# The down projection's seven products in the order 1 5 6 3 2 7 4, with the norms of the first token half issued in steps among the last two

## The chip, the cores and the metric

The kernel runs on one core of a Trainium2 chip. The metric is the device time of one execution in microseconds (us). A core has a matrix engine (TensorE, PE in the profile; PEld is its weight load), a vector engine (VectorE, DVE), a scalar engine (ScalarE, ACT), GpSimd (POOL) and a queue engine for transfers (SyncE, SP). They run side by side, each through its own list of instructions in order, and wait for one another through semaphores.

## The reference, cut to what matters

One layer of a decoder trunk, 512 tokens wide 1024, in float32:

```python
h = swiglu(rms_norm(x, ffn1_pre), ffn1_w_gu, ffn1_w_down)     # D_FF = 2816
x = x + 0.5 * rms_norm(h, ffn1_post)
h = token_mixer(rms_norm(x, mix_pre), ...)                    # pooling groups and sliding-window attention
x = x + rms_norm(h, mix_post)
h = swiglu(rms_norm(x, ffn2_pre), ffn2_w_gu, ffn2_w_down)
x = x + 0.5 * rms_norm(h, ffn2_post)

def rms_norm(x, g):  return x * rsqrt(mean(x * x, -1) + EPS) * g
def swiglu(h, w_gu, w_down):
    gate, up = split(h @ w_gu, 2);  return (silu(gate) * up) @ w_down
```

## The kernel before

**Precision.** A float32 product is made of three fp32r matmuls (`mm3`, L357 to L361): every operand is split into a high part (a cast on ACT) and a low part (a subtraction on DVE), and high x high, high x low and low x high are summed. So each chunk of weights costs a cast `f_d_hi` (L166) on ACT and a subtraction `f_d_lo` (L169) on DVE, and each operand made of activations costs the same (`f1e_hi`, `f1e_lo` at L635 and L636; the names begin with f1 in the first FFN and f2 in the second).

**The down projection** (`down_proj`, L616) multiplies 512 tokens x 2816 by 2816 x 1024. Both are cut in halves, and the four output quarters come from seven products in place of eight (Strassen's way with Winograd's sums). The products have numbers; `PRODUCTS` (L39) is their order, 1 5 6 3 7 2 4 before. A product covers 256 tokens (two blocks of 128, t = 0 and 1) by 512 columns, with an inner length of 1408: 11 slices of 128, in six chunks of weights (five of two slices, the last of one). A slice is three matmuls for each of the two blocks, so a product is 66 matmuls of 512 columns.

The products accumulate in PSUM banks, one for each block: 1, 6, 7 and 4 in `xs_` (f_x in the profile), one on top of the other, 5 and 3 in `ys` (f_y), and 2 in `zs_` (f_z). What the sums need from an intermediate state is taken off by `put_away` (L654): after 1, 5 and 6 copies on ACT, after 3, 7 and 2 a DVE instruction for each block. At the end the first token half (blocks 0 and 1) has its two column halves in kept[1] (the first product plus product 2) and kept[6]; the second half (blocks 2 and 3) has them in xs_ after product 4 and in kept[5].

The activations' operand for product i is made by `form(i, g)` in three groups g (two of four slices, one of three). For 5, 6, 3 and 7 a DVE instruction first combines two quarters in place (L626 to L632); for 1, 2 and 4 there is none. Then ACT casts and DVE subtracts.

**Order.** Inside `in_order()` PE, DVE, ACT and POOL run exactly in program order. For product i and chunk n that order is: weights of the chunk three ahead (cast and subtraction), at n = 0, 2, 4 the forming of a group of the next product, the chunk's matmuls, and at n = 0 the put-away of the product before. The weights' parts have six buffers, so the cast of a chunk waits until PE is through with the chunk six before it. Outside `in_order()` PE is still in program order, but DVE, ACT and POOL are placed by a planner. SP issues the transfers in program order.

**The end of the down projection.** Before the change `in_order()` covers the first six products. Then come two chunks of product 4 for both blocks, put_away(2) after the first, `normed(0)` and `normed(1)`; the other four chunks (the tail) run once for block 0 and once for block 1, each followed by `normed(2)` or `normed(3)`.

`normed(t)` (L672) is `post_norm` (L407): two squares with sums on ACT (`squares`, L353), the mean on DVE (L339), the root on POOL (L334), two multiplies by the gain on DVE (L413) that for t < 2 write in place over what the squares read, and two updates of x on DVE (L416). In the second FFN each update is followed by its transfer to the output on SP (L418). After that `done(t)` is called: nothing in the second FFN; in the first it is `done1` (L842), which is the mixer's `pre_norm` (L383) of the new x: squares on ACT, mean, root, two DVE instructions that write `xn_b` (L378).

`between(t)` is `between1` (L846) in the first FFN: eight transposes of xn_b on PE (`tr_mx`, L391) for t = 0 and 1, and copies of high and low parts into `xT` (L397 on ACT, L400 on DVE). Before the change between(0) comes between the two runs of the tail, and between(1) after the second chunk of block 1's run. The mixer then starts with `qkv_block(0)`: 24 matmuls of pq for block 0 of the tokens (xT and the weights wq), then 24 half as wide of pkv (weights wkv, cast when pkv asks for them).

Of the kernel before, what the change touches and what calls it, by code (L numbers as in the profile page):

```python
# [33 lines left out]
EPS = 1e-6  # L34
# [1 line left out]
CH = 256  # L36
NCH = FF // CH
TAIL = 4
PRODUCTS = (1, 5, 6, 3, 7, 2, 4)  # L39
BLOCKS = {1: (0, 0), 2: (1, 0), 3: (1, 1)}  # L40
CW = 256 + 16 * NG + 8
WB = 6
# [25 lines left out]
def trunk_layer(  # L68
# [37 lines left out]
    def in_order():  # L106
        return tc.manual_schedule(engines={E.PE, E.DVE, E.Activation, E.Pool})

    def bank(name):
        return banks_of["pool"].tile([P, 512], F32, tag="ps", name=name)  # L110
# [4 lines left out]
    def slot(name, shape=(P, 512), dtype=F32):  # L115
        return slots_of["pool"].tile(list(shape), dtype, tag="h", name=name)
# [67 lines left out]
    W = Weights()  # L184
# [50 lines left out]
    def add_ffn(name, w_gu, w_down):  # L235
        for c in range(NCH):
            add_gate_up(name, w_gu, c)
        cut = w_down[0].rearrange("(q j p) n -> j p q n", j=2, p=P)
        for i in PRODUCTS:
            for q in range(0, NCH, 2):  # L240
# [90 lines left out]
    def power(ms, name):  # L331

        r = sm.tile([P, 1], F32, tag="r", name=f"r_{name}")
        nc.gpsimd.tensor_tensor(r, ms, half, ALU.pow)  # L334
        return r

    def mean_square(ss2, eps, name):
        ms = sm.tile([P, 1], F32, tag="ms", name=f"ms_{name}")
        nc.vector.scalar_tensor_tensor(ms, ss2[:, 0:1], eps, ss2[:, 1:2], ALU.add, ALU.add)  # L339
        return ms  # L340
# [30 lines left out]
    def sizes(t, name, split=False):  # L371
        return squares([xs[t][:, :512], xs[t][:, 512:]], ROOT, f"{name}{t}", split)

    def scaled(t, r, g, name, between=lambda: None, xn=None):
        xn = xn or [slot(f"xn_{name}{t}{n}") for n in range(2)]
        for n in range(2):
            at = slice(n * 512, (n + 1) * 512)
            nc.vector.scalar_tensor_tensor(xn[n], xs[t][:, at], r, g[n], ALU.mult, ALU.mult)  # L378
            if n == 0:
                between()  # L380
        return xn

    def pre_norm(t, g, name, xn=None):  # L383
        r = power(mean_square(sizes(t, name), EPS, f"{name}{t}"), f"{name}{t}")
        return scaled(t, r, g, name, xn=xn)

    def transposes(t, xn, xT, name):
        for h in range(2):
# [15 lines left out]
    def halves(g):  # L404
        return g[:, :512], g[:, 512:]

    def post_norm(t, parts, tmp, g, scale, name, dst=None):  # L407

        ss2 = squares(parts, ROOT / scale, f"{name}{t}")
        r = power(mean_square(ss2, EPS / (scale * scale), f"{name}{t}"), f"{name}{t}")  # L410
        for n in range(2):
            at = slice(n * 512, (n + 1) * 512)
            nc.vector.tensor_tensor(tmp[n], parts[n], g[:, at], ALU.mult)  # L413
        for n in range(2):
            at = slice(n * 512, (n + 1) * 512)
            nc.vector.scalar_tensor_tensor(xs[t][:, at], tmp[n], r, xs[t][:, at], ALU.mult, ALU.add)  # L416
            if dst is not None:
                nc.sync.dma_start(dst[:, at], xs[t][:, at])  # L418
# [197 lines left out]
    def down_proj(name, hs, ends, g_post, between, done):  # L616

        forms = {}  # L620

        def form(i, g):

            a11, a21, a12, a22 = (hs[g][:, f] for f in range(4))
            if i == 5:
                nc.vector.tensor_tensor(a21, a22, a21, ALU.subtract)  # L626
            elif i == 6:
                nc.vector.scalar_tensor_tensor(a11, a21, -1.0, a11, ALU.mult, ALU.subtract)
            elif i == 3:
                nc.vector.scalar_tensor_tensor(a21, a11, -1.0, a12, ALU.mult, ALU.subtract)  # L630
            elif i == 7:
                nc.vector.scalar_tensor_tensor(a11, a11, -1.0, a22, ALU.mult, ALU.subtract)  # L632
            src = {1: a11, 5: a21, 6: a11, 3: a21, 7: a11, 2: a12, 4: a22}[i]
            hi, lo = act_pair(f"{name}e{i}{g}", src.shape)
            nc.scalar.copy(hi, src)  # L635
            nc.vector.tensor_tensor(lo, src, hi.bitcast(F32), ALU.subtract)  # L636
            forms[i, g] = hi, lo

        ys, zs_, xs_ = ([bank(f"{name}_{b}{t}") for t in range(2)] for b in "yzx")
        fresh = {1: xs_, 5: ys, 2: zs_}  # L640
        into = {**fresh, 6: xs_, 3: ys, 7: xs_, 4: xs_}
        kept = {}

        def multiply(i, n, w, blocks=(0, 1)):
            for q in range(2 * n, min(2 * n + 2, NCH)):
                hh, hl = forms[i, q // 4]
                for t in blocks:
                    at = (slice(None), q % 4, slice(t * P, (t + 1) * P))
                    mm3(
                        into[i][t], (hh[at], hl[at]), tuple(part[:, q % 2] for part in w),  # L650
                        i in fresh and q == 0, q == NCH - 1, True,
                    )

        def put_away(i):  # L654

            if i in (1, 5):
                kept[i] = wk.tile([P, 2, 512], F32, tag="sg2", bufs=2, name=f"{name}_p{i}")
                for t in range(2):
                    nc.scalar.copy(kept[i][:, t], into[i][t])
            elif i == 6:  # L660
                kept[i] = [slots_of["pool"].tile([P, 512], F32, tag="k", bufs=2, name=f"{name}_p6{t}") for t in range(2)]
                for t in range(2):
                    nc.scalar.copy(kept[i][t], xs_[t])
            for t in range(2):
                if i == 3:
                    nc.vector.scalar_tensor_tensor(kept[6][t], ys[t], -1.0, kept[6][t], ALU.mult, ALU.subtract)
                elif i == 7:
                    nc.vector.scalar_tensor_tensor(kept[5][:, t], xs_[t], -1.0, kept[5][:, t], ALU.mult, ALU.subtract)
                elif i == 2:
                    nc.vector.tensor_tensor(kept[1][:, t], zs_[t], kept[1][:, t], ALU.add)  # L670

        def normed(t):  # L672
            first = kept[1][:, t] if t < 2 else xs_[t - 2]
            second = kept[6][t] if t < 2 else kept[5][:, t - 2]
            dst = out[0, t * P : (t + 1) * P, :] if name == "f2" else None
            tmp = slots_of["pool"].tile([P, 512], F32, tag="k", bufs=2, name=f"{name}_n{t}") if t >= 2 else first
            post_norm(t, [first, second], [tmp, second], g_post, 0.5, f"{name}po", dst)
            done(t)

        NW = (NCH + 1) // 2  # L680
        with behind(ends[0]):
            form(1, 0)
            form(1, 1)
        with behind(ends[1]):
            form(1, 2)
            W.get(f"{name}_d10")
        with in_order():
            for at, i in enumerate(PRODUCTS[:-1]):
                for n in range(NW):
                    w = W.get(f"{name}_d{i}{n}")  # L690
                    if n % 2 == 0:
                        form(PRODUCTS[at + 1], n // 2)
                    multiply(i, n, w)
                    if n == 0 and at:
                        put_away(PRODUCTS[at - 1])
        i = PRODUCTS[-1]
        for n in range(2):
            multiply(i, n, W.get(f"{name}_d{i}{n}"))
            if n == 0:
                put_away(PRODUCTS[-2])  # L700
        normed(0)
        normed(1)
        tail = [W.get(f"{name}_d{i}{n}", 0) for n in range(2, NW)]
        if name == "f1":
            W.run_ahead = 3
            W.more(2)
        for t in range(2):
            for n, w in enumerate(tail):
                multiply(i, n + 2, w, (t,))
                if t and n == 1:  # L710
                    between(1)
            if t and name == "f1":
                W.more(2)
            normed(t + 2)
            if t == 0:
                between(0)
        use_slots(f"{name}_end", HB)


# [67 lines left out]
    ends = gate_up("f1", xq, hs, first_steps)  # L787
    g2 = gain(ffn1_post, "g2")
    g3 = halves(gain(mix_pre, "g3"))
# [16 lines left out]
    late = ExitStack()  # L806
# [33 lines left out]
    xns = {}  # L840

    def done1(t):  # L842
        xn = ap.tile([P, 2, 512], F32, tag=("ahi", "alo")[t % 2], name=f"xn_b{t}")
        xns[t] = pre_norm(t, g3, "b", [xn[:, n] for n in range(2)])

    def between1(t):  # L846
        if t == 0:
# [364 lines left out]
    def normed(t):  # L1212
        later["x", t] = scaled(t, later["r", t], g5, "c")
# [68 lines left out]
    hs2 = []  # L1282
    ends = gate_up("f2", xq2, hs2, last_steps)
    g6 = gain(ffn2_post, "g6")
    down_proj("f2", hs2, ends, g6, lambda t: None, lambda t: None)


# [27 lines left out]
```

## Time and profile before

| | |
|---|---|
| median of three runs | 872.73 us (870.80 to 873.77) |
| the profiled execution, its own time | 870.79 us |
| its span in the profile | 869.0 us |
| PE busy, share of the span | 829.5 us, 95% |
| DVE busy | 686.1 us, 79% |
| ACT busy | 447.0 us, 51% |
| POOL busy | 234.1 us, 27% |
| mean granted clock of TensorE | 0.981 |

The first FFN's down projection lies from about 249 to 362 us of the span, the second's from about 752 to 862. Busy times are of engines that work side by side. A matmul row's duration reaches past the start of the next one, since matmuls are pipelined; the distance from start to start is what a matmul costs. In a timeline the brackets hold the idle time of the engine before the row and what ended it.

### The profile page before, as it was taken

The numbers are of one execution on the slowest core, as the hardware profiler recorded it, in microseconds if no ns is written. First come the engines' busy times: TensorE is split into PE (matmuls) and PEld (weight loads), VectorE is DVE, ScalarE is ACT, GpSimd is POOL, SyncE is SP. The second block draws the span as 40 slices with busy tenths as digits, with TensorE's granted clock in tenths as the row PEclk, the third lists the DMA queues.
The fourth block names the chain that finished last, engine by engine and source line by source line (L and its number), as shares of the span: only waits on it lengthen the run. The fifth ranks groups of instructions, "written<-read, shape, count | busy, mean of one in ns | idle before, by whom it ended". The sixth has DMA issues, their size and how long they took to land. (4 is left out here: it accounts for less than half of the span.)

```text
span 869.0 us, 13979 instructions
## 1 busy us (share of the span) xinstructions
PE 829.5 (95%) x5501; PEld 757.1 (87%) x5501; DVE 686.1 (79%) x875; ACT 447.0 (51%) x699; POOL 234.1 (27%) x304
## 2 busy tenths in 40 slices
PE   8989999999999999799988986999999999999996
PEld 6989999999988878588866876999999999988785
DVE  6968887778987798745898879677888888877895
ACT  5544444454555575445664254544554445555662
POOL 4103334433310000123564433023333333300001
PEclk9999999999999999899999999999999999999999
DMA  9327888888885567312004304149899988865542
GB/s 307 116 72 216 228 234 220 226 235 238 228 264 180 181 199 250 108 49 50 25 25 145 97 7 139 52 163 228 228 241 240 233 234 227 235 214 175 175 160 97
DMA packets 96876, 150.77 MB, mean 173 GB/s; under 512 B 6948, under 2 KB 53676, under 8 KB 96812
## 3 DMA queue, kind: packets, MB, share of 16 engines
q1 hardware_dynamic: 77100, 103.74, 37.4%
q0 software_dynamic: 19712, 46.15, 22.7%
q8 instruction: 43, 0.70, 0.3%
q14 instruction: 21, 0.17, 0.1%
HBM read 147.77 MB, written 48.23 MB: 226 GB/s over the span
## 5 line engine op out<-in xcount | busy, mean ns | idle before, releaser
L571 POOL DMA_DIRECT2D f_t<-in_ffn_w_down x132 | 89.6, 753 | 81.5 <-issue 49.8
L169 DVE TENSOR_TENSOR f_d_lo<-f_d_raw,f_d_hi 128x1024 fp32r<-128x1024 f32 x84 | 92.2, 1131 | 8.9 <-ACT f_d_hi L166 8.2
L166 ACT CAST f_d_hi<-f_d_raw 128x1024 fp32r<-128x1024 f32 x84 | 79.0, 978 | 15.7 <-PE f_z L361 14.4
L568 POOL COPY f_k<-f_h 1x1 f32<-1x1 f32 x18 | 21.0, 1164 | 178.0 <-DVE f_h L560 178.0
L595 ACT COPY f_h<-f_y 128x512 f32<-128x512 f32 x20 | 11.7, 587 | 80.9 <-PE f_y L361 80.9
L603 ACT ACTIVATE f_s<-f_s 128x1024 f32<-128x1024 f32 x20 | 21.2, 1060 | 41.5 <-DVE f_s L602 41.5
L571 POOL DMA_DIRECT2D f_t<-f_t x44 | 32.2, 801 | 37.2 <-issue 28.1
L600 ACT COPY f_s<-f_x 128x512 f32<-128x512 f32 x20 | 11.7, 587 | 48.4 <-PE f_x L361 48.4
L635 ACT CAST f2e_hi<-f_h 128x1024 fp32r<-128x1024 f32 (+1 forms) x21 | 20.4, 976 | 30.9 <-DVE f_h L632 7.7
L635 ACT CAST f1e_hi<-f_h 128x1024 fp32r<-128x1024 f32 (+1 forms) x21 | 20.4, 977 | 30.8 <-DVE f_h L632 7.7
L359 PE MATMUL f_x<-f_d_hi,f1e_hi 128*128 128x512 f32 x88 | 35.1, 399 | 1.2 <-DVE f_h L611 1.2
L360 PE MATMUL f_x<-f_d_lo,f1e_hi 128*128 128x512 f32 x88 | 34.8, 396 | 0.5 <-DVE f_d_lo L169 0.5
L360 PE MATMUL f_x<-f_d_lo,f2e_hi 128*128 128x512 f32 x88 | 34.4, 391 | 0.8 <-DVE f_d_lo L169 0.8
L359 PE MATMUL f_x<-f_d_hi,f2e_hi 128*128 128x512 f32 x88 | 34.4, 390 | 0.7 <-DVE f_h L611 0.7
L361 PE MATMUL f_x<-f_d_hi,f1e_lo 128*128 128x512 f32 x88 | 34.6, 393 | 0.0
L361 PE MATMUL f_x<-f_d_hi,f2e_lo 128*128 128x512 f32 x88 | 34.3, 390 | 0.0
L334 POOL TENSOR_TENSOR r_f1po<-ms_f1po,half 128x1 f32<-128x1 f32 x4 | 3.5, 866 | 108.7 <-DVE ms_f1po L339 108.7
L636 DVE TENSOR_TENSOR f1e_lo<-f_h,f1e_hi 128x1024 fp32r<-128x1024 f32 (+1 forms) x21 | 23.7, 1132 | 11.4 <-ACT f1e_hi L635 11.4
L636 DVE TENSOR_TENSOR f2e_lo<-f_h,f2e_hi 128x1024 fp32r<-128x1024 f32 (+1 forms) x21 | 23.6, 1134 | 11.4 <-ACT f2e_hi L635 11.4
L334 POOL TENSOR_TENSOR r_f2po<-ms_f2po,half 128x1 f32<-128x1 f32 x4 | 3.5, 867 | 106.0 <-DVE ms_f2po L339 106.0
L587 ACT COPY f_s<-f_x 128x512 f32<-128x512 f32 x20 | 11.7, 587 | 36.9 <-PE f_x L361 34.2
L359 PE MATMUL po<-wo_hi,yT_hi 128*128 128x512 f32 x64 | 25.9, 405 | 0.0
(1029 smaller groups left out, 3458.0 us busy)
## 6 DMA issues: line engine op xcount, KB each, us to landing
f_t<-in_ffn_w_down POOLq DMA_DIRECT2D x132, 256.0 KB, 6.3
f_d_raw<-f_t SPq DMA_DIRECT2D x40, 512.0 KB, 4.6
f_d_raw<-in_ffn_w_down SPq DMA_DIRECT2D x30, 512.0 KB, 4.4
f_t<-f_t POOLq DMA_DIRECT2D x44, 256.0 KB, 6.6
f_raw<-in_ffn_w_gu SPq DMA_DIRECT2D x8, 512.0 KB, 7.9
x<-in_x SPq DMA_DIRECT2D x4, 512.0 KB, 8.3
f_d_raw<-f_t SPq DMA_DIRECT2D x8, 256.0 KB, 3.7
wq_raw<-in_w_in SPq DMA_DIRECT2D x4, 512.0 KB, 4.3
```

The lines of the kernel that those rows point to most:

```text
L166: nc.scalar.copy(hi, src)
L169: self.lo.tensor_tensor(lo, src, hi.bitcast(F32), ALU.subtract)
L359: nc.tensor.matmul(ps, wh, xh, start=first, stop=False, skip_group_check=open_)
L360: nc.tensor.matmul(ps, wh, xlo, start=False, stop=False, skip_group_check=open_)
L361: nc.tensor.matmul(ps, wlo, xh, start=False, stop=last, skip_group_check=open_)
L568: then = nc.gpsimd.tensor_copy(tick, hs[(c - 1) // 4][:1, 0, (c - 1) % 4, :1]).ins
L571: nc.gpsimd.dma_start(to, part, accum_op=op, max_dma_last_dim=2048)
L587: on_act.append(nc.scalar.copy(sg[:, :, a], px[:, :, a]).ins)
L595: on_act.append(nc.scalar.copy(h[1], py[:, :, a]).ins)
L603: on_act.append(nc.scalar.activation(sg, sg, AF.Silu, scale=-1.0).ins)
L635: nc.scalar.copy(hi, src)
L636: nc.vector.tensor_tensor(lo, src, hi.bitcast(F32), ALU.subtract)
```

## The change

Products 7 and 2 change places. Product 4 now follows 7 on the same banks, so the last two chunks of product 7 run first for block 0 and then for block 1, each followed by its own put_away(7, (t,)). The norms of blocks 0 and 1 become generators: `normed(0)` is started after the first chunk of product 7, `normed(1)` after the third, and `step()` issues the next part of each behind every chunk, until the first two chunks of product 4 are through. The parts are: squares and gain multiplies; mean and root; updates of x, with `done`'s squares; mean and root of `pre_norm`; xn_b. All of it now lies inside `in_order()`. Where two steps and a put-away meet, the steps' instructions come first. The gain multiplies are issued before the mean in place of after it. In the tail between(0) and between(1) each come after the second chunk of their own block's run.

```diff
-PRODUCTS = (1, 5, 6, 3, 7, 2, 4)
+PRODUCTS = (1, 5, 6, 3, 2, 7, 4)
...
-    def pre_norm(t, g, name, xn=None):
-        r = power(mean_square(sizes(t, name), EPS, f"{name}{t}"), f"{name}{t}")
-        return scaled(t, r, g, name, xn=xn)
+    def pre_norm(t, g, name, xn):
+        ss2 = sizes(t, name)
+        yield
+        r = power(mean_square(ss2, EPS, f"{name}{t}"), f"{name}{t}")
+        yield
+        scaled(t, r, g, name, xn=xn)
...
         ss2 = squares(parts, ROOT / scale, f"{name}{t}")
-        r = power(mean_square(ss2, EPS / (scale * scale), f"{name}{t}"), f"{name}{t}")
         for n in range(2):
             at = slice(n * 512, (n + 1) * 512)
             nc.vector.tensor_tensor(tmp[n], parts[n], g[:, at], ALU.mult)
+        yield
+        r = power(mean_square(ss2, EPS / (scale * scale), f"{name}{t}"), f"{name}{t}")
+        yield
...
-            post_norm(t, [first, second], [tmp, second], g_post, 0.5, f"{name}po", dst)
-            done(t)
+            yield from post_norm(t, [first, second], [tmp, second], g_post, 0.5, f"{name}po", dst)
+            yield from done(t)
...
+        steps = []
+
+        def step():
+            for s in steps:
+                next(s, None)
+
         with in_order():
             for at, i in enumerate(PRODUCTS[:-1]):
                 for n in range(NW):
                     w = W.get(f"{name}_d{i}{n}")
                     if n % 2 == 0:
                         form(PRODUCTS[at + 1], n // 2)
+                    if i == 7 and n >= NW - 2:
+                        continue
                     multiply(i, n, w)
+                    step()
                     if n == 0 and at:
                         put_away(PRODUCTS[at - 1])
-        i = PRODUCTS[-1]
-        for n in range(2):
-            multiply(i, n, W.get(f"{name}_d{i}{n}"))
-            if n == 0:
-                put_away(PRODUCTS[-2])
-        normed(0)
-        normed(1)
+                    if i == 7 and n in (0, 2):
+                        steps.append(normed(n // 2))
+            late = [W.get(f"{name}_d7{n}") for n in (NW - 2, NW - 1)]
+            for t in range(2):
+                for n in range(2):
+                    multiply(7, NW - 2 + n, late[n], (t,))
+                step()
+                put_away(7, (t,))
+            i = PRODUCTS[-1]
+            for n in range(2):
+                w = W.get(f"{name}_d{i}{n}")
+                for t in range(2):
+                    multiply(i, n, w, (t,))
+                step()
+            for s in steps:
+                for _ in s:
+                    pass
         tail = [W.get(f"{name}_d{i}{n}", 0) for n in range(2, NW)]
...
         for t in range(2):
             for n, w in enumerate(tail):
                 multiply(i, n + 2, w, (t,))
-                if t and n == 1:
-                    between(1)
+                if n == 1:
+                    between(t)
             if t and name == "f1":
                 W.more(2)
-            normed(t + 2)
-            if t == 0:
-                between(0)
+            for _ in normed(t + 2):
+                pass
```

More of the change, by code (lines that the diff above doesn't have):

```diff
@@ L652, in multiply, with put_away @@
                     )
-        def put_away(i):
+        def put_away(i, blocks=(0, 1)):
             if i in (1, 5):
@@ L663, in put_away @@
                     nc.scalar.copy(kept[i][t], xs_[t])
-            for t in range(2):
+            for t in blocks:
                 if i == 3:
@@ L843, in done1 @@
         xn = ap.tile([P, 2, 512], F32, tag=("ahi", "alo")[t % 2], name=f"xn_b{t}")
-        xns[t] = pre_norm(t, g3, "b", [xn[:, n] for n in range(2)])
+        xns[t] = [xn[:, n] for n in range(2)]
+        return pre_norm(t, g3, "b", xns[t])
     def between1(t):
@@ L1284, in trunk_layer @@
     g6 = gain(ffn2_post, "g6")
-    down_proj("f2", hs2, ends, g6, lambda t: None, lambda t: None)
+    down_proj("f2", hs2, ends, g6, lambda t: None, lambda t: ())
 _INS = [
```

## The prediction

> **What bounds the kernel now.** I read the page first (span), then TensorE's waits, then windows around the longest of them, then the timelines of PE, DVE and ACT there. Times below are us from the span's start; a window's row gives start:end, length, busy time of PE, PEld, DVE, ACT and POOL, granted clock, DMA share, GB/s.
>
> ```profile
> span 869.0 us, 13979 instructions
> ```
> ```profile
> 47.00:51.00 4.00, 3.97 (x21) 4.00 (x22) 1.23 (x1) 0.93 (x1) 0.00 (x0) 0.57 0.11 25
> 327.00:342.00 15.00, 15.00 (x67) 12.41 (x67) 13.13 (x16) 7.99 (x11) 0.00 (x0) 1.00 0.80 267
> 349.74:373.37 23.63, 17.39 (x62) 13.22 (x61) 17.61 (x33) 13.22 (x33) 4.98 (x6) 0.78 0.31 100
> 373.37:400.00 26.63, 26.63 (x179) 23.98 (x178) 9.86 (x34) 9.93 (x32) 4.78 (x11) 1.00 0.16 40
> ```
> ```profile
> PE tr_mx L391 <- DVE xn_b L378: 3.9, 1, 3.9
> ...
> PE pq L361 <- DVE xT_lo L400: 1.2, 1, 1.2
> PE pq L359 <- ACT xT_hi L397: 1.1, 1, 1.1
> ```
>
> The second and fourth windows show PE without a gap, inside a down projection and in the mixer after it: the kernel is bound by TensorE there, and time comes only from its gaps. The third window, the end of the first FFN's down projection up to the mixer's K/V projection, is 23.63 long with a clock of 0.78, and the three waits lie in it. DVE is busy 13.13 of 15.00 in the second window: close behind PE. The fence after this has PE's rows: the start of product 7 in each FFN, the start of product 4 in the first, and the 3.9 us wait.
>
> ```profile
> 308.82 0.39 PE L359 MATMUL f_x<-f_d_hi,f1e_hi 128*128 128x512 f32 x1
> 309.70 0.50 PE L360 MATMUL f_x<-f_d_lo,f1e_hi 128*128 128x512 f32 x1 [0.49 <-DVE f_d_lo L169]
> 310.03 0.39 PE L361 MATMUL f_x<-f_d_hi,f1e_lo 128*128 128x512 f32 x1
> ...
> 339.53 0.39 PE L359 MATMUL f_x<-f_d_hi,f1e_hi 128*128 128x512 f32 x1
> ...
> 357.42 1.78 PE L391 MATMUL tr_mx<-ident,xn_b 128*128 128x128 f32 x8 [3.91 <-DVE xn_b L378]
> 358.84 0.78 PE L359 MATMUL f_x<-f_d_hi,f1e_hi 128*128 128x512 f32 x1
> ...
> 361.92 0.39 PE L361 MATMUL f_x<-f_d_hi,f1e_lo 128*128 128x512 f32 x1
> ...
> 815.36 0.39 PE L359 MATMUL f_x<-f_d_hi,f2e_hi 128*128 128x512 f32 x1
> 816.55 0.50 PE L360 MATMUL f_x<-f_d_lo,f2e_hi 128*128 128x512 f32 x1 [0.81 <-DVE f_d_lo L169]
> 816.90 0.40 PE L361 MATMUL f_x<-f_d_hi,f2e_lo 128*128 128x512 f32 x1
> ```
>
> Products 7 and 2 take 339.53 - 308.82 = 30.71, less the stall at their start (310.03 - 308.82 - 2 x 0.227 = 0.75): 29.96 for 132 matmuls, 0.227 each, 15.0 a product, 1.36 for six matmuls (a chunk of weights for one token block).
>
> **The gain: what the long window holds.** At 0.227 its work is 45 matmuls (21 of the tail's second block, 24 of pq: 10.2) and two sets of eight transposes at some 0.8 to 0.9: 12.0. It takes 23.63, so 11.65 are lost to waits and the slow clock. After the change xn_b0 and xn_b1 are made before the tail, and the transposes of block 0 move into the tail of block 0; pq then finds its xT ready. If nothing else is late, all 11.65 go. Product 2 in place of 7 after product 3 also takes three combinations (L632) out of DVE's list while product 3 runs, so the stalls at product 7's start go: 0.75 in the first FFN and 816.90 - 815.36 - 0.45 = 1.1 in the second. Together 13.5. This is the ceiling.
>
> **The loss: DVE at the new boundary from 7 to 4.** Both products write xs_. Product 4's first matmul on a block must wait until put_away(7) has read that block. Before, product 2 (bank zs_) lay between and hid it for 15 us. Now the cover is nine matmuls (2.05) for block 0 and six (1.36) for block 1, and DVE and ACT run in program order, so put_away stands behind all that the steps issue. How far is DVE behind by then?
>
> ```profile
> 298.95 1.22 DVE L632 SCALAR_TENSOR_TENSOR f_h<-f_h 128x1024 f32<-128x1024 f32 x1
> 301.28 1.23 DVE L636 TENSOR_TENSOR f1e_lo<-f_h,f1e_hi 128x1024 fp32r<-128x1024 f32 x1 [1.11 <-ACT f1e_hi L635]
> 303.20 1.23 DVE L169 TENSOR_TENSOR f_d_lo<-f_d_raw,f_d_hi 128x1024 fp32r<-128x1024 f32 x1 [0.70 <-ACT f_d_hi L166]
> ...
> 315.78 1.22 DVE L636 TENSOR_TENSOR f1e_lo<-f_h,f1e_hi 128x1024 fp32r<-128x1024 f32 x1
> 316.92 1.28 DVE L666 SCALAR_TENSOR_TENSOR f_p<-f_y,f_p 128x512 f32<-128x512 f32 x2
> ...
> 805.80 1.22 DVE L632 SCALAR_TENSOR_TENSOR f_h<-f_h 128x1024 f32<-128x1024 f32 x1
> ```
>
> One product's list on DVE with combinations goes from 298.95 to 315.78: 16.8 against PE's 15.0. A combination costs 301.28 - 298.95 = 2.33 with the wait for ACT (1.9 for the shorter third). A low part costs 316.92 - 315.78 = 1.14 (half a chunk 0.6, a third group 0.87), a pair of put-aways 1.2. Without the combinations (6.5) and most of the 0.70 wait the list takes 9.9: after the change DVE is at 308.8 when PE starts product 2 at 308.8. The list of product 2's time has the combinations again: 16.8 - 0.7 + 1.2 (put_away(3)) + 1.1 (first low part of form 4) = 18.4, to 327.2. PE ends product 2 at 323.8, call it T. So put_away(2) starts at T+3.3. In the second FFN DVE's 805.80 stands 9.56 before product 7, in the first 298.95 stands 9.87 before: 0.3 later, T+3.6.
>
> The steps' prices:
>
> ```profile
> 340.26 0.62 ACT L353 ACTIVATE j_f1po<-f_p 128x512 bf16<-128x512 f32 x1
> 340.79 0.19 ACT L353 ACTIVATION_READ_ACCUMULATOR j_f1po<-f_p 128x1 f32 x1
> 341.01 0.63 ACT L353 ACTIVATE j_f1po<-f_p 128x512 bf16<-128x512 f32 x1
> ```
> ```profile
> 342.60 0.15 DVE L339 SCALAR_TENSOR_TENSOR ms_f1po<-ss_f1po 128x1 f32<-128x1 f32 x1
> 342.67 0.68 DVE L413 TENSOR_TENSOR f_p<-f_p,g 128x512 f32<-128x512 f32 x1
> 343.80 0.75 DVE L416 SCALAR_TENSOR_TENSOR x<-f_p,r_f1po,x 128x512 f32<-128x512 f32 x1 [0.46 <-POOL r_f1po L334]
> ```
>
> A square with its read is 0.75 on ACT; mean, POOL's root and the way back 1.2 (342.60 to 343.80); a gain multiply 0.6, an update 0.67; ACT can square the new x when its first half is written, 0.75 after the update begins (0.1 more taken for the signal).
>
> First FFN, DVE from T+3.3: put_away(2) to 4.5; low of chunk 7.4 to 5.6; two gain multiplies to 6.8; half chunk 7.5 to 7.4; form 4's second low to 8.5; mean; low of 4.0 to 9.75; updates of block 0 to 11.1. ACT now squares x (10.65 to 12.1) and then block 1's two parts (to 13.6), and the multiplies write in place, so DVE waits 1.75 and ends them at 14.2. Chunk 4.1 waits 0.4 for its cast behind those squares: 15.8; form 4's third low 16.7; chunk 4.2 17.8; two means; put_away(7,0) 17.95 to 18.6. PE, through with product 7 at T+15.0, resumes at 18.7. DVE goes on with two xn_b (their root has just come) to 20.0 and two updates of block 1 to 21.4, and put_away(7,1) ends at 22.0. Block 1 of product 4 starts at 22.05 where it would at 15.0 + 1.36 = 16.4: 5.7 lost. With every wait of DVE taken out it would be 3.2, and since a wait can't be below nothing and the list is in the program, I exclude a gain; a further cast or DMA late adds up to 1.
>
> Second FFN, the same list without xn_b and its squares, so without DVE's 1.75 wait: put_away(7,0) from T+15.85 to 16.5, a stall of 1.6; the two updates 17.0 to 18.3; put_away(7,1) to 19.0: 2.7 lost (0 without the backlog, 3.5 with one more late cast). Its outputs of block 0 and 1 enter SP's queue ahead of the last weight loads; chunk 4.5 is wanted some 8 us after the boundary, so I cost that at nothing; uncovered it would show as PE waiting for a cast.
>
> **The clock.** The 3.9 wait was followed by eight matmuls from 358.84 to 361.92, 3.08 for 1.82: 1.25 lost. I take this for the first FFN (between nothing, as slow matmuls inside DVE's stall are free, and 2.5, as its second stall can bring it twice). For the second, stalls of 1.6 and 1.1 lie between the rows of 0.49 and 0.81 above, at full speed after 310.03 and 816.90, and this one:
>
> ```profile
> 47.03 0.36 PE L359 MATMUL f_y<-f1t_hi,f_1p_hi 128*128 128x256 f32 x1 [2.24 <-ACT f_s L587]
> ```
>
> After 2.24 of waiting the window 47:51 has a clock of 0.57, 4.00 x 0.43 = 1.7 lost. I take half, 0.9. The Trainium skill (TensorE: Matmul & The Clock Gate, section "Why this matters for your kernels") says the clock falls for PE-idle gaps above about 3 us. By that rule the second FFN's stalls cost no clock and the sum would be 0.9 lower; the 2.24 row above is against it.
>
> **What is late next.** The mixer's K/V weights:
>
> ```profile
> 370.72 1.99 ACT L166 CAST wkv_hi<-wkv_raw 128x1024 fp32r<-128x1024 f32 x2
> ```
> ```profile
> 371.80 2.60 DVE L169 TENSOR_TENSOR wkv_lo<-wkv_raw,wkv_hi 128x1024 fp32r<-128x1024 f32 x2 [1.64 <-ACT wkv_hi L166]
> ```
>
> The tail ended at 361.92 + 0.39 = 362.3 = E, the casts began at E+8.4, behind x of block 3, and pkv started at 373.37, just after the first low part. After the change pq starts at E, so pkv wants it at E+5.5. With the order kept but the transposes' copies gone from between, block 3's norm gives x at E+3.5, its square ends at E+4.3, wph 4.8, the cast 5.8, the low part 7.0: 1.5 of waiting (0 if the cast is placed ahead, 5.1 if it stays at E+8.4).
>
> **Sum.** Gains 11.65 + 0.75 + 1.1 = 13.5. Losses 5.7 + 1.25 + 1.5 (first FFN) and 2.7 + 0.9 (second) = 12.05. Net -1.45. The span's 869.0 goes to 867.6, the profiled execution's own 870.79 to 869.3. That execution stands 1.94 below the median of 872.73; the median goes to 871.3. The end of the kernel (block 3's norm after the last matmul) is untouched.
>
> **Rivals.**
> *DVE has no backlog at T.* DVE's 13.13 of 15.00 in the second window speaks for it, the sum of lists above against. If put_away(2) starts within about 1 us of T, everything is 2.5 to 4 earlier: the first stall goes, the second in the first FFN falls to about 1.7, the second FFN loses nothing. 13.5 - 1.7 - 1.5 = 10.3: 862.4.
> *Slower: K/V casts stay late.* Outside the hand-written order DVE and ACT are placed by a planner. If wkv_hi keeps its E+8.4, pkv waits 5.1, and the clock falls (1.7 as at 47:51): 3.6 + 1.7 over the forecast, +3.85: 876.6. It decides from a wait of about 4 us with its clock. For it: its start at E+8.4 shows that in this trace the planner put it behind block 3's norm. Against: part of what stood ahead of it, the transposes' copies, is gone from there.
> *The norms aren't within the products.* DVE so late that xn_b1 comes with the tail again; then the 3.9 wait returns with its 1.25 of slow clock, -1.45 + 5.15 = +3.7: 876.4. Against: xn_b1 is due at T+27, its transposes some 7 us later.
>
> **Chances.** Forecast's case (DVE late at the boundary, 867 to 874.5): 0.58; no backlog: 0.22; K/V late: 0.13; moot or other placements in the mixer: 0.07. The forecast's case crosses the limit of 0.3% (2.6 us, about what a measurement tells from no change): I give 0.2 of its 0.58 to below 870.1, 0.33 to within and 0.05 to above. Faster 0.22 + 0.2 = 0.42; slower 0.13 + 0.05 + 0.02 = 0.20; same 0.38. Range 862 to 876.5: it takes in most of the no-backlog case and the K/V case up to its price; the forecast's case alone is 867 to 874.5.
>
> **What would show it.** Right: PE idle ahead of product 4's first f_x matmul on each block, released by DVE's subtraction of put_away(7) (L668 before), about 3.6 and 1 us in the first FFN and 1.6 and 1.1 in the second; no wait at tr_mx; no stall at the start of product 2; pkv held by wkv_lo. Wrong: put_away(2) on DVE early after product 2's end, or PE waits in the mixer that are not there now.

## The result and the profile after

| | before | after |
|---|---|---|
| median | 872.44 us (10 runs, 867.90 to 873.77) | 876.61 us (10 runs, 874.68 to 878.31) |
| profiled execution, its own time | 870.79 us | 878.00 us |
| mean granted clock of TensorE | 0.981 | 0.981 |

The ratio of after to before is 1.0054, with an interval of 1.0036 to 1.0073: slower by 0.54%, some 4.7 us (the two medians lie 4.2 apart). The profiled executions lie 7.2 apart, because that of before is 1.65 below its median and that of after 1.4 above. After's ten times lie in two groups, 874.68 to 875.17 and 876.59 to 878.31, and the trace is of the longer one. Sums below are made between these two executions.

The page of after, its span and its busy times, and TensorE's waits (us in total, times, longest):

```profile
span 876.2 us, 13988 instructions
PE 829.2 (95%) x5501; PEld 756.6 (86%) x5501; DVE 686.1 (78%) x875; ACT 446.0 (51%) x699; POOL 234.6 (27%) x304
```
```profile
PE f_x L359 <- DVE f_p L674: 8.2, 4, 4.2
...
PE pkv L359 <- ACT wkv_hi L166: 2.1, 1, 2.1
PE f_x L359 <- DVE f_h L547: 1.9, 1, 1.9
...
PE pkv L360 <- DVE wkv_lo L169: 1.1, 1, 1.1
```

The busy times are those of before within 1 us, so the loss is again in PE's gaps. The waits of before at tr_mx, pq and f_d_lo are gone. Four kinds are in their place: put_away(7) (`f_p`, now L674), the two of the K/V weights, and one that the prediction does not have, `f_x` behind `f_h` of L547, which is in the gate/up products of the second FFN, some 190 us behind the moved transposes.

The same rows in PE's timeline, with the first matmul of product 7 above them:

```profile
323.86 0.39 PE L359 MATMUL f_x<-f_d_hi,f1e_hi 128*128 128x512 f32 x1
...
343.18 0.47 PE L359 MATMUL f_x<-f_d_hi,f1e_hi 128*128 128x512 f32 x1 [4.20 <-DVE f_p L674]
346.49 0.80 PE L359 MATMUL f_x<-f_d_hi,f1e_hi 128*128 128x512 f32 x1 [1.22 <-DVE f_p L674]
...
371.82 0.38 PE L359 MATMUL pkv<-wkv_hi,xT_hi 128*128 128x256 f32 x1 [2.09 <-ACT wkv_hi L166]
373.30 0.39 PE L360 MATMUL pkv<-wkv_lo,xT_hi 128*128 128x256 f32 x1 [1.10 <-DVE wkv_lo L169]
...
552.24 0.64 PE L492 MATMUL f_c<-f2b_lo,f_c_hi 128*128 128x256 f32 x4
554.80 0.35 PE L359 MATMUL f_x<-f2b_hi,f_1p_hi 128*128 128x256 f32 x1 [1.92 <-DVE f_h L547]
...
851.23 0.47 PE L359 MATMUL f_x<-f_d_hi,f2e_hi 128*128 128x512 f32 x1 [2.36 <-DVE f_p L674]
853.28 0.79 PE L359 MATMUL f_x<-f_d_hi,f2e_hi 128*128 128x512 f32 x1 [0.43 <-DVE f_p L674]
```

And windows of after around or behind the waits of `f_x` (columns as in the prediction; the clock is the third number from the end):

```profile
338.90:351.00 12.10, 6.67 (x18) 4.78 (x18) 10.60 (x16) 6.70 (x11) 2.46 (x3) 0.72 0.43 121
346.49:364.13 17.64, 17.64 (x76) 14.58 (x77) 12.57 (x19) 11.03 (x23) 1.94 (x2) 0.87 0.54 172
554.80:560.00 5.20, 5.20 (x31) 5.20 (x32) 0.00 (x0) 0.52 (x2) 0.00 (x0) 0.67 0.31 101
851.00:857.00 6.00, 5.34 (x17) 4.01 (x17) 4.97 (x7) 0.00 (x0) 0.17 (x1) 0.72 0.23 87
```

How the 7.2 come about, by the start of the same matmul in both executions. At the second matmul of pkv, after stands at 373.30, and before stood one matmul behind its 373.37: the first FFN has given its whole gain back and ends level. At the second FFN's first f_x of the gate/up products, 554.80 stands against 552.72 in before: 1.92 of that is the wait. With the slow clock behind it (0.67 over 5.20 us, 1.7 lost) this makes 3.6. PE's row of before there has no wait:

```profile
552.72 0.28 PE L359 MATMUL f_x<-f2b_hi,f_1p_hi 128*128 128x256 f32 x1
```

The rest up to here is the same in both: PE's last `f_c` group starts at 552.24, and DVE's two readings of the gate/up tiles (`f_h`) at 553.37. From the first to the last f_x of the second down projection it is 754.32 to 861.16 in before, 106.84, and 757.94 to 868.13 in after, 110.19: another 3.35.

### The profile page after: what moved, and what is told of

Read it like the earlier page. It is cut to its first block, busy times and chain, and to the rows that moved or that the text cites. A ratio compares the mean times of both kernels' runs of the same rounds, so it can differ in the third digit from the quotient of the medians.

```text
span 876.2 us, 13988 instructions
## 1 busy us (share of the span) xinstructions
PE 829.2 (95%) x5501; PEld 756.6 (86%) x5501; DVE 686.1 (78%) x875; ACT 446.0 (51%) x699; POOL 234.6 (27%) x304
## 5 line engine op out<-in xcount | busy, mean ns | idle before, releaser
L601 ACT COPY f_h<-f_y 128x512 f32<-128x512 f32 x20 | 11.7, 587 | 80.9 <-PE f_y L361 80.9
L606 ACT COPY f_s<-f_x 128x512 f32<-128x512 f32 x20 | 11.7, 587 | 48.5 <-PE f_x L361 48.5
L642 DVE TENSOR_TENSOR f1e_lo<-f_h,f1e_hi 128x1024 fp32r<-128x1024 f32 (+1 forms) x21 | 23.7, 1133 | 11.4 <-ACT f1e_hi L641 11.4
L642 DVE TENSOR_TENSOR f2e_lo<-f_h,f2e_hi 128x1024 fp32r<-128x1024 f32 (+1 forms) x21 | 23.6, 1134 | 11.4 <-ACT f2e_hi L641 11.4
L593 ACT COPY f_s<-f_x 128x512 f32<-128x512 f32 x20 | 11.7, 586 | 40.5 <-PE f_x L361 37.9
L359 PEld LDWEIGHTS f_x<-f_d_hi,f1e_hi 128*128 128x128 f32 x88 | 17.1, 194 | 11.3 <-issue 4.6
```

Source lines behind the costliest of these rows:

```text
L359: nc.tensor.matmul(ps, wh, xh, start=first, stop=False, skip_group_check=open_)
L593: on_act.append(nc.scalar.copy(sg[:, :, a], px[:, :, a]).ins)
L601: on_act.append(nc.scalar.copy(h[1], py[:, :, a]).ins)
```

## The experiments

The theory (A): product 4 waits for put_away(7) because DVE comes to it late, the K/V weights are cast behind block 3's norm, and the wait at `f_h` is a matter of PSUM banks. In the built programs the second FFN's last gate/up tile, read by DVE until 554.65, lies in bank 5 in before and in bank 1 in after; the first `f_x` takes banks 0 and 1 in both. Which bank a tile gets depends on the order in which the tiles before it were asked for and given back, and the moved transposes change that order: in order_only below, whose transposes stand where before had them, the four gate/up tiles lie in the same banks as in before. (The first of the four lies in bank 0 in after, and in bank_moved as well, where no wait is left; it is the last one that counts.) Rivals: the new order of the products costs by itself (B); the wait at `f_h` is one of timing, because the first FFN leaves other things late (C).

Each ratio is to before on the same chip.

**bank_moved.** After, with one matmul of a single column into a bank of its own, ahead of the second FFN's gate/up block (1, 0). Its result is used by nothing; it only changes the banks that the tiles behind it get, and the last tile comes to lie in bank 5.

```diff
         if (i, kh) == (1, 0):
+            for i_ in range(1):
+                nc.tensor.matmul(bank(f"rot{i_}")[:, :1], sqp[:, :P], ones, start=True, stop=True)
             turn_late(2)
```

> The changed kernel with one tiny matmul (one column, into a bank of its own) ahead of the second FFN's second gate block. It does nothing but shift which PSUM banks the second FFN's four gate/up tiles get: the one read last by DVE moves from bank 1 to bank 5, off the pair (0, 1) of the first pair tile f_x. Theory A (the 1.92 us wait at 554.8 and the slow clock behind it come from that bank): the wait is gone, the span is 3.6 us shorter than the changed kernel's 876.2, the ratio to before falls from 1.0054 to about 1.001. Rival C (the wait is a matter of timing in that execution or of the planner's order on DVE): the wait stays, about 1.9, and the ratio stays near 1.005.

Measured: 872.77 us, ratio 1.0015 (0.9998 to 1.0031), against 1.0054 for after. The window at that place in before and in bank_moved:

```profile
552.00:560.00 8.00, 8.00 (x69) 8.00 (x68) 3.88 (x5) 2.85 (x4) 0.00 (x0) 1.00 0.26 72
```
```profile
552.00:560.00 8.00, 8.00 (x69) 8.00 (x68) 3.54 (x5) 4.01 (x5) 0.00 (x0) 1.00 0.43 133
```

PE has no gap there again, while the waits at product 4 (4.17 and 0.42, 2.36 and 0.41) and at pkv (2.08 and 1.10) stay. (The 0.42 was 1.22 in after, but block 1 starts 3.31 behind block 0 in both: here the matmuls ahead of the wait ran slower.) So the bank alone carries some 0.4% of after's 0.54% (the two intervals do not overlap).

**before_bad_bank, before_bad_bank_2, before_bank_control.** The same idle matmul in before, once, twice and three times. By the built programs the last tile then lies in bank 0, 1 and 7.

```diff
         if (i, kh) == (1, 0):
+            for i_ in range(1):    # 2 and 3 in the other kernels
+                nc.tensor.matmul(bank(f"rot{i_}")[:, :1], sqp[:, :P], ones, start=True, stop=True)
             turn_late(2)
```

> The kernel before with the same tiny matmul at the same place. Here it moves the tile read last by DVE from bank 5 to bank 0, onto the first pair. Theory A: a wait of about 1.9 us at the first f_x matmul of the second FFN appears, with a slow clock behind it, and the kernel is 3.6 us slower than before: ratio 1.004. Rival C: no wait there, ratio 1.000.

> The kernel before with two tiny matmuls, which put the tile that DVE reads last on bank 1, on the first pair. Theory A: the wait at the first f_x matmul of the second FFN is there, 0.8 to 1.9 us, ratio 1.002 to 1.004. Rival C: 1.000.

> The kernel before with three tiny matmuls at the same place, which leave the tile that DVE reads last on bank 7, off the first pair. A control for the one matmul that put it on bank 0 (1.0017). Theory A: no wait at the first f_x matmul of the second FFN, ratio 1.000 (within 0.001). If the matmuls or the shift as such cost time, 1.002 or more.

Measured: 873.69 us, 1.0017 (1.0002 to 1.0032); 874.29 us, 1.0020 (1.0005 to 1.0035); 870.08 us, 0.9988 (0.9970 to 1.0007). The wait appears in both kernels whose tile shares a bank with `f_x`, and not in the control. Rival C falls as the cause of the wait: nothing of the first FFN differs here. But the wait is smaller than in after, 0.78 and 0.88, and the loss with it, 0.2% where 0.4% was expected of before_bad_bank. PE's row of before_bad_bank, and DVE's rows there and in after:

```profile
556.04 0.39 PE L359 MATMUL f_x<-f2b_hi,f_1p_hi 128*128 128x256 f32 x1 [0.78 <-DVE f_h L541]
```
```profile
553.57 0.68 DVE L541 SCALAR_TENSOR_TENSOR f_h<-f_c,f_s 128x512 f32<-128x512 f32 x1
555.29 0.69 DVE L541 SCALAR_TENSOR_TENSOR f_h<-f_c,f_s 128x512 f32<-128x512 f32 x1 [1.04 <-PE f_c L486]
```
```profile
552.23 1.22 DVE L169 TENSOR_TENSOR f_1p_lo<-f_1a_raw,f_1p_hi 128x1024 fp32r<-128x1024 f32 x1
553.37 1.28 DVE L547 SCALAR_TENSOR_TENSOR f_h<-f_c,f_s 128x512 f32<-128x512 f32 x2
```

In before_bad_bank DVE is idle 1.04 and reads the bank the moment PE is done: 0.78 is about the price of one reading. In after PE is through at 552.88 (552.24 + 0.64), but DVE is still with a low part and reads both tiles from 553.37: 1.92. DVE begins its readings at nearly the same time in both (553.57 and 553.37); it is PE that comes 2.4 later in before_bad_bank, where its clock from 540.00 on was 0.84, against 1.00 in after. Behind the wait of 0.78 no matmul is slow (0.12 apart from the second on), behind the 1.92 the clock is 0.67. So the sharing of a bank costs 0.8 to 3.6 us here, by which of PE and DVE comes first; this spread is read from the rows, no run isolates it.

**putaway_first.** After, with put_away(7, (t,)) ahead of the steps. By the built program the last gate/up tile still lies in bank 1, as in after; the wait there is 0.88 in the traced execution, without a slow clock behind it (1.00).

```diff
-                step()
                 put_away(7, (t,))
+                step()
```

> The changed kernel with put_away(7, (t,)) issued ahead of step() in the two late halves of product 7. Theory A (DVE's place in its list makes the waits at the boundary from 7 to 4): the second wait of each FFN (1.22 and 0.43 us) goes, the first ones stay within 0.3 of 4.2 and 2.4, since DVE is late by what stands ahead of both; 1.5 to 3 us faster than the changed kernel, ratio to before about 1.003. Rival B (the wait is that of product 4 behind product 7 on the same banks, whatever the steps do): both waits of each FFN stay, ratio 1.005.

Measured: 872.95 us, 1.0030 (1.0011 to 1.0050), about as expected; the interval overlaps that of after, so the gain itself is not clear of the noise. The waits of block 1 are gone in both FFNs; those of block 0 stay, 4.0 and 2.3, as TensorE's waits in putaway_first show (put down there to the small mean on DVE that runs just before PE resumes):

```profile
PE f_x L359 <- DVE ms_f1po L339: 4.0, 1, 4.0
PE f_x L359 <- DVE ms_f2po L339: 2.3, 1, 2.3
```

So xn_b and the updates of block 1 held block 1's put-away, as the prediction had it, and block 0's is held by what DVE has in its list from earlier, not by the step next to it.

**order_only.** The new order and the split put-away, with the norms and the transposes where before had them.

```diff
-                    if i == 7 and n in (0, 2):
-                        steps.append(normed(n // 2))
...
-                step()
-            for s in steps:
-                for _ in s:
-                    pass
+        for t in range(2):
+            for _ in normed(t):
+                pass
...
-                if n == 1:
-                    between(t)
+                if t and n == 1:
+                    between(1)
...
+            if t == 0:
+                between(0)
```

> The new order of products and the split put_away(7) kept, no steps: the norms of blocks 0 and 1 and the transposes stand where they stood before the change. Theory A: DVE reaches put_away(7, 0) before PE has left the block, so no wait over 0.3 us at the boundary from 7 to 4; the stalls of 0.75 and 1.1 at the start of the product after 3 go; the 3.9 us wait of the transposes stays. 1.9 us faster than before: ratio 0.998. Rival B: waits of 1 us or more per block stay at the boundary from 7 to 4 in both FFNs, ratio 1.002 or more.

Measured: 870.39 us, 0.9993 (0.9975 to 1.0011), 0.998 was expected, and the interval holds both that and no change. PE's rows with a wait of order_only, from the boundary to the mixer's start and in the second FFN:

```profile
354.24 1.31 PE L395 MATMUL tr_mx<-ident,xn_b 128*128 128x128 f32 x8 [0.77 <-DVE xn_b L378]
363.21 0.79 PE L359 MATMUL pq<-wq_hi,xT_hi 128*128 128x512 f32 x1 [5.60 <-ACT xT_hi L401]
365.25 0.80 PE L361 MATMUL pq<-wq_hi,xT_lo 128*128 128x512 f32 x1 [0.82 <-DVE xT_lo L404]
...
848.83 0.50 PE L359 MATMUL f_x<-f_d_hi,f2e_hi 128*128 128x512 f32 x1 [0.74 <-DVE f_p L674]
```

Product 4 waits for nothing in the first FFN and 0.74 in the second, more than the 0.3 allowed but not the 1 us per block in both of rival B. Rival B falls: without the steps DVE is in time for put_away(7), though it reads the very banks that product 4 writes. The wait of before at the transposes did not stay as expected; it went to pq, behind the transposes' copies on ACT.

**kv_early, before_kv_early.** After with the bank moved, and before, each with the K/V weights asked for (`W.more(4)` in place of 2) ahead of block 3's norm.

```diff
             if t and name == "f1":
-                W.more(2)
+                W.more(4)
```

> The changed kernel with the steps as they are, the tiny matmul that moves the bank, and the K/V weights made ahead of block 3's norm. Theory A: the waits at the boundary from 7 to 4 stay (4.2, 1.2, 2.4, 0.4), pkv's waits of 2.1 and 1.1 go; 3 us faster than the changed kernel with the bank moved alone (1.0015): ratio 0.998. Rival D: the two waits come back at another instruction of the mixer, ratio 1.0015.

> The kernel before with the K/V weights made ahead of block 3's norm. In the trace of before pkv started without a wait, PE having been late itself. Theory A: nothing to gain there, ratio 1.000 (within 0.002). If the early casts alone made the kernel faster, it would show here as 0.997 or less.

Measured: kv_early 868.78 us, 0.9968 (0.9948 to 0.9988); before_kv_early 874.63 us, 1.0029 (1.0012 to 1.0046). In kv_early pkv starts at 369.34 without a wait (bank_moved: 370.80, then its second matmul at 372.29), while product 4's waits stay (4.18 and 0.96, 2.36 and 0.43). The interval lies below that of bank_moved. So the K/V wait is due to the casts' place. In before the same edit costs, and was expected to cost nothing: PE's rows of before_kv_early show the early casts ahead of the transposes' copies, for which pq waits (2.47 and 2.08, against 1.10 and 1.23 in before):

```profile
365.51 0.50 PE L359 MATMUL pq<-wq_hi,xT_hi 128*128 128x512 f32 x1 [2.47 <-ACT xT_hi L397]
368.32 0.79 PE L361 MATMUL pq<-wq_hi,xT_lo 128*128 128x512 f32 x1 [2.08 <-DVE xT_lo L400]
```

**steps_late.** After with fewer steps ahead of put_away(7): put_away first, no step behind the chunks n = 3 of product 7, and `normed(1)` begun only after put_away(7, (1,)). The bank is moved as well (by the matmul of bank_moved, not shown again).

```diff
-                    step()
+                    if n < 3:
+                        step()
...
-                    if i == 7 and n in (0, 2):
-                        steps.append(normed(n // 2))
+                    if i == 7 and n == 0:
+                        steps.append(normed(0))
...
-                step()
                 put_away(7, (t,))
+                if t:
+                    steps.append(normed(1))
+                step()
```

> The changed kernel with less for DVE ahead of put_away(7): block 0's norm gets only its first two steps within product 7 (chunks 1 and 2), put_away(7, (t,)) comes ahead of the steps, x of block 0 comes behind put_away(7, block 0), and block 1's norm starts behind put_away(7, block 1). Also the tiny matmul that moves the bank. Theory A (DVE's list sets the loss at the boundary): the waits at the boundary fall from 4.2, 1.2, 2.4 and 0.4 to 0.5 or less each; the second FFN's down projection takes about 1 us less than before; in the first, pq starts near 356 in place of 363.4, pkv then waits for its weights (cast behind block 3's norm) 2 to 3 us and starts near 364 in place of 373.4. In all some 10 us faster than before: ratio 0.989. Rival D (the mixer's start is set by something else, so that time won in the first down projection is given back in full): pkv starts no earlier than 370, ratio 0.996 or more.

Measured: 867.35 us, 0.9958 (0.9940 to 0.9977); 0.989 was expected. DVE's and then PE's rows of steps_late:

```profile
337.11 0.69 DVE L674 SCALAR_TENSOR_TENSOR f_p<-f_x,f_p 128x512 f32<-128x512 f32 x1
339.14 0.69 DVE L674 SCALAR_TENSOR_TENSOR f_p<-f_x,f_p 128x512 f32<-128x512 f32 x1
```
```profile
368.62 0.58 PE L359 MATMUL pkv<-wkv_hi,xT_hi 128*128 128x256 f32 x1 [6.86 <-ACT wkv_hi L166]
370.10 0.58 PE L360 MATMUL pkv<-wkv_lo,xT_hi 128*128 128x256 f32 x1 [0.90 <-DVE wkv_lo L169]
```

The put-aways come at 337.11 and 339.14 (342.35 and 345.75 in after) and no wait of product 4 is left. PE reaches the mixer 8.0 sooner, pq at 356.16 against 364.13, and gives most of it back at pkv, where it waits 7.8 in place of the 2 to 3 expected: the cast of wkv_hi starts at 367.52 against 370.73 in after, only 3.2 sooner. It starts 11.4 behind pq, later still than the 8.4 of the prediction's slower rival, and the wait is 7.8 where that rival had 5.1. The ratio is all but rival D's 0.996; but pkv starts before 370, and the next kernel shows that it is the casts that hold it.

**steps_late_kv_early, kv_early_bad_bank.** The former is steps_late with `W.more(4)`; the latter the same without the idle matmul, which puts the last gate/up tile back into bank 1.

```diff
             if t and name == "f1":
-                W.more(2)
+                W.more(4)
...
         if (i, kh) == (1, 0):
-            for i_ in range(1):       # the second kernel only
-                nc.tensor.matmul(bank(f"rot{i_}")[:, :1], sqp[:, :P], ones, start=True, stop=True)
```

> The same, and four weights in place of two are made ahead of block 3's norm, so that the K/V weights' casts and subtractions come before it. Theory A: no wait of pkv over 0.5, pkv starts near 361.5, 2.5 us faster than the same without it: ratio 0.985. Rival D: no more than the same without it.

> The kernel with late steps and early K/V weights (ratio 0.9855) without the tiny matmul, so that the gate/up tile that DVE reads last is again on bank 1, on the first pair. Theory A: a wait of 0.8 to 2 us at the first f_x matmul of the second FFN and a slow clock behind it, 2 to 3.5 us slower than with the matmul: ratio 0.988 to 0.9895. Rival C: no difference, 0.9855.

Measured: 859.12 us, 0.9855 (0.9830 to 0.9880), and 861.79 us, 0.9883 (0.9865 to 0.9901). Rows of steps_late_kv_early on ACT and PE, and two of its windows, from product 4 to pkv:

```profile
355.34 2.00 ACT L166 CAST wkv_hi<-wkv_raw 128x1024 fp32r<-128x1024 f32 x2 [0.45 <-PE f_x L361]
```
```profile
361.28 0.28 PE L359 MATMUL pkv<-wkv_hi,xT_hi 128*128 128x256 f32 x1
```
```profile
338.90:351.00 12.10, 12.10 (x59) 10.12 (x58) 10.26 (x15) 9.70 (x22) 3.81 (x3) 1.00 0.58 180
351.00:361.28 10.28, 10.25 (x48) 8.07 (x48) 10.08 (x19) 7.52 (x17) 2.97 (x2) 1.00 0.62 210
```

PE runs through at full clock and pkv starts at 361.28, 12.1 sooner than in before. Its span is 857.3, 11.7 below that of before. This kernel is faster than both, by 1.5% (1.2 to 1.7) than before. So the gain that the prediction counted was there: the 12.1 at pkv stand against its 11.65 + 0.75 for the first FFN, and the second FFN's down projection takes 105.5 from its first `f_x` to its last, 1.3 less than in before, against its 1.1. In kv_early_bad_bank PE's row shows the bank once more, with a wait between the two sizes above (the two ratios differ as expected, but their intervals overlap):

```profile
543.53 0.35 PE L359 MATMUL f_x<-f2b_hi,f_1p_hi 128*128 128x256 f32 x1 [1.15 <-DVE f_h L547]
```

## Why the prediction was wrong

The forecast was 871.3 us, no change; measured is 876.61, slower, 0.1 above the range. Against the profiled execution the forecast was -1.45 and the row sums give +7.2. The parts:

**The gain** was right: the waits at tr_mx and pq and the stalls at the start of product 7 are gone. So was the reading that DVE is late. DVE's rows of after:

```profile
327.23 1.28 DVE L676 TENSOR_TENSOR f_p<-f_z,f_p 128x512 f32<-128x512 f32 x2
...
337.37 1.45 DVE L416 TENSOR_TENSOR f_p<-f_p,g 128x512 f32<-128x512 f32 x2 [1.70 <-ACT j_f1po L353]
...
342.35 0.68 DVE L674 SCALAR_TENSOR_TENSOR f_p<-f_x,f_p 128x512 f32<-128x512 f32 x1
343.10 1.42 DVE L378 SCALAR_TENSOR_TENSOR xn_b<-x,r_b,g 128x512 f32<-128x512 f32 x2
344.43 1.41 DVE L422 SCALAR_TENSOR_TENSOR x<-f_p,r_f1po,x 128x512 f32<-128x512 f32 x2
345.75 0.69 DVE L674 SCALAR_TENSOR_TENSOR f_p<-f_x,f_p 128x512 f32<-128x512 f32 x1
367.36 0.15 DVE L339 SCALAR_TENSOR_TENSOR ms_f1po<-ss_f1po 128x1 f32<-128x1 f32 x1
367.43 1.40 DVE L378 SCALAR_TENSOR_TENSOR xn_b<-x,r_b,g 128x512 f32<-128x512 f32 x2
368.75 0.74 DVE L422 SCALAR_TENSOR_TENSOR x<-f_n,r_f1po,x 128x512 f32<-128x512 f32 x1
```

With T = 323.86, put_away(2) is at T+3.4 (forecast T+3.3), DVE's wait for the squares is 1.70 (1.75), put_away(7, (0,)) is at T+18.5 (T+17.95), xn_b and the updates stand between the two put-aways as listed. Most of the half microsecond is a wait of DVE for POOL's root that the list did not have:

```profile
332.81 1.41 POOL L334 TENSOR_TENSOR r_f1po<-ms_f1po,half 128x1 f32<-128x1 f32 x1 [89.01 <-DVE ms_f1po L339]
334.26 1.41 DVE L422 SCALAR_TENSOR_TENSOR x<-f_p,r_f1po,x 128x512 f32<-128x512 f32 x2 [0.46 <-POOL r_f1po L334]
```

The root took 1.41 here and 0.87 in before, where POOL had idled even longer (97.48). Why, no run shows. The rival without a backlog is refuted. In the second FFN the waits are 2.36 and 0.43, 2.8, where 2.7 was forecast; that the sum agrees so well is in part luck, since 1.6 and 1.1 were forecast for the two blocks.

**Steps that failed.**

1. *The sum left out the second FFN's gate/up products.* "What is late next" was asked only of the mixer's weights, not of where the program's tiles come to lie. Moving the transposes moved the banks: +3.6 in the profiled execution, 0.4% by bank_moved. This is the largest part, and no case of the prediction holds it.
2. *"Block 3's norm gives x at E+3.5 ... 1.5 of waiting".* With E = 364.1, where pq starts, x starts at 368.75, E+4.6: on DVE the mean comes only at 367.36, and two xn_b of block 2 stand between it and x. The cast of wkv_hi starts at 370.73, E+6.6, in place of E+4.8. pkv waits 2.09, then 1.10 for the low part, and its second matmul comes 3.6 later than if pq had run into it: +2.1 over the forecast.
3. *The clock of the first FFN, 1.25.* From block 1's first matmul to pq, 346.49 to 364.13, it takes 17.64 for some 15.4 of work at 0.227: 2.2, so +1.0. The two waits of 4.20 and 1.22 came together and matmuls stayed 0.43 apart until 350.9. The forecast had named 2.5 as the upper end, for a second stall that brings the slow clock twice.
4. *The first boundary, 5.7.* Block 1's first matmul is at 346.49 where T+16.4 is 340.26: 6.2, +0.5.
5. *The second FFN, net +2.5.* 2.8 of waits, 1.7 of slow clock (0.72 over 6 us) and 1.1 gained give 3.4; measured 3.35, +0.85. In bank_moved and kv_early, with the same waits but no slow clock behind them, the stretch takes 108.84, 2.0 more than in before.

Together 3.6 + 2.1 + 1.0 + 0.5 + 0.85 = 8.05 of the 8.65 that lie between -1.45 and +7.2. The rest is not resolved.

The slower rival named 876.6, the time measured, but that is chance: K/V casts that stay late put 2.1 on the forecast here, where the rival has 5.3. In steps_late, where the boundary is mended, pkv's wait of 7.8 is the main loss that is left.

The Trainium skill (TensorE: Matmul & The Clock Gate, section "Why this matters for your kernels") has the clock fall for gaps above about 3 us. Here it fell behind waits of 1.92 (0.67 after it) and 2.36 (0.72). The price of 0.9 taken against that rule was too small in this execution, not too large; in bank_moved, where the clock did not fall behind the same 2.36, it was too large.

## What to carry to other kernels

When work is moved ahead in an engine that runs in program order, put first what frees the resource that another engine is about to need (here the bank), then what feeds the next stage, and then the rest; when one wait goes, look up the next operand on the path (here the K/V weights) and move its preparation in the same edit, since of the two edits here (kv_early and steps_late, both with the bank moved) each alone ended 0.3% and 0.4% below before, and both together 1.5%. Before costing an edit as local, list which PSUM bank every later stage's first tiles take: a tile that moves to another bank can put a wait nearly 200 us away.

## What the runs showed of the hardware

The clock's answer to a wait differs between executions of nearly the same program. The wait at product 4 in the second FFN is 2.36 and 0.43 in after and 2.36 and 0.41 in bank_moved. The windows behind it, of after (851.00:857.00, above, clock 0.72) and of bank_moved:

```profile
846.00:852.00 6.00, 5.59 (x25) 4.28 (x24) 4.09 (x5) 0.00 (x0) 0.00 (x0) 1.00 0.23 87
```

At 1.00 the same wait cost next to nothing in clock. Nor did 2.09 and 1.10 at pkv in after, by its window there:

```profile
371.82:379.00 7.18, 6.08 (x41) 5.55 (x42) 5.41 (x9) 3.88 (x10) 2.99 (x7) 1.00 0.00 1
```

But behind the same two waits at pkv (2.08 and 1.10) the clock was 0.70 over 5.7 us in bank_moved (from 372.29) and in putaway_first (from 371.30). The four lone waits at the banks, 0.78 to 1.15, were followed by a clock of 1.00 over the next 5.2 us; 1.10 and 1.23 a microsecond apart, at pq in before, were not (matmuls 0.43 apart from 365.96 to 371.5), but there a wait of 3.91 with its own slow stretch had ended only 2 us ahead. What decides it, no run here tells.

It is worth about 1.7 us an event, and is probably part of why executions of one kernel differ by up to 6 us: in the 35 executions of before that stand beside bank_moved, the four shortest (867.67 to 868.45) have a mean clock of 0.985 to 0.987, the four longest (873.16 to 873.48) of 0.975 to 0.979. It is not all: in after the four shortest have the lower clock, 0.978, and five of the six others 0.981 or 0.982.
